# Input projection of a hybrid encoder layer: weights asked for a block ahead, square-sum rows asked for later, pooling products a block later

## The chip, the cores and the metric

The kernel runs on one core of a Trainium2 chip. The metric is the device time of one execution in microseconds (us). The engines are named as in the profile: PE (TensorE, matrix products), PEld (its weight loads), DVE (VectorE), ACT (ScalarE), POOL (GpSimd), SP (SyncE, which here only issues DMAs).

## The reference

One encoder layer over 2048 positions of width 1024: a mixer, a cross-attention into 256 memory rows, and a gated feed-forward part. The change lies in the first part of the mixer, its input projection:

```
z  = rmsnorm(x) @ w_in + b_in          # 2048 x 1024 times 1024 x 2176
za = z[:, :768]      -> gelu, split u and v, rmsnorm of v per head,
                        128-position gating with w_s       (gMLP heads)
zb = z[:, 768:1024]  -> centred average pooling, 4 windows, minus zb,
                        then @ w_pool, + b_pool, * pool_scale
zc = z[:, 1024:]     -> q, k, v of the dilated window attention
```

Everything is float32. A float32 product is made of three products: each operand is split into a rounded high part and a low part (the rest), and high x high, high x low and low x high are added up.

## The kernel before, in words

`mix_in` is the input projection. The positions are cut into 4 chunks `c` of 512. For each chunk the scaled input, transposed, lies in `hth` and `htl` (high and low part, `load_x`). The columns of `w_in` are worked off in this order, where 0 to 7 are blocks of 128 columns (`t_block`) and `None` stands for the 384 columns of the attention's v (`v_rows`):

```
ORDER = ((0, 1, 4, 7, 3, 6, 2, 5, None), (0, 1, 4, 7, None, 3, 6, 2, 5))
```

The first tuple is chunk 0's, the second that of chunks 1 to 3; `b` is the place in it. Blocks 0 and 1 are the pooling heads, 2 to 7 q and k. The gMLP products (`za`) stand in front of place 0 in chunks 1 to 3 and in front of place 7 (`ZB`) in chunk 0. One block is 24 products on PE (8 steps over the 1024, three products each, L115, L116 and L117 in `mm3`: `wth` x `hth`, `wth` x `htl`, `wtl` x `hth`).

A block's weights come in three steps: SP issues a DMA of 512 KB into `st` (two buffers), POOL makes the high part `wth` (L95), DVE the low part `wtl` (L99). `wth` and `wtl` have two buffers each (`a_wt`), so the weights of one block take the place of those of the block two loads earlier, and POOL's L95 waits until PE has done the last product with them. The eight gMLP weight tiles `wa10` to `wa13` and `wa00` to `wa03` come the same way, through the same `st`, but stay (`load_gmlp`).

A block's result `pz` (five PSUM buffers) is multiplied by the spread norms `rb` on DVE and gets its bias on ACT (`t_out`). `rb` comes from the sums of squares of the rows of x (`row_squares`: four DMAs of 512 KB into `xr`, which has two buffers, squared on ACT) by way of `stats`: a reciprocal root on DVE, four products `pt<-diag,ones` on PE (L87), a copy on ACT.

Pooling of a quarter of a chunk pair (`pooling`: DMA of `z`, sums on POOL, split into `pzsh` and `pzsl`) is written one place ahead of its six products `pp` (`pooled`).

Each engine works its own instructions in a fixed order. That order is not the order of the code: a scheduler lays the program out from its own estimates and from the buffers, and `tc.issue_after(x)` marks work that it may not put ahead of instruction x. So the tables below show the order that came out.

Of the kernel before, what the change touches and what calls it, by code (L numbers as in the profile page):

```python
# [12 lines left out]
AF = mybir.ActivationFunctionType  # L13
# [106 lines left out]
class Ffn:  # L120
# [160 lines left out]
    ORDER = [f + v for f in range(0, NF, 2) for v in (0, NF)]  # L281
# [278 lines left out]
ZB = 7  # L560
ORDER = ((0, 1, 4, 7, 3, 6, 2, 5, None), (0, 1, 4, 7, None, 3, 6, 2, 5))
# [3 lines left out]
def mix_in(cx, x_r, x_t, gn, w_t, b_t, w_v, b_v, w_a, b_a, v_g, w_s, b_s, rel, onehot, mrow, tt, pw, pb, psc, edge, invw, zt, vt, yt):  # L565
# [4 lines left out]
    tc, nc = cx.tc, cx.nc  # L570
    AH = 6
    AW = 384
    with ExitStack() as es:
# [6 lines left out]
        wtp = pool("a_wt", 2)  # L580
# [12 lines left out]
        def load_w(pl, tag, src, n=D, **k):  # L593
            st = stp.tile([P, D], F32, name="st", tag="st")
            nc.sync.dma_start(st[:, :n], src)
            return cx.split_w(pl, st[:, :n], tag, tag, n, **k)

        def load_x(c):

            cs = slice(c * 512, (c + 1) * 512)  # L600

            xs = hp.tile([P, KD, 512], F32, name="xs", tag="hth") if c == 0 else None
            hi = hp.tile([P, KD, 512], F32R, name="hth", tag="hth")
            lo = hp.tile([P, KD, 512], F32R, name="htl", tag="htl")
            for k in range(KD):
                xt = xp.tile([P, 512], F32, name="xt", tag="xt") if c else xs[:, k]
                nc.sync.dma_start(xt, x_t[k * P:(k + 1) * P, cs])
                last = nc.scalar.activation(hi[:, k], xt, AF.Copy, scale=gk[:, k:k + 1])
                nc.vector.scalar_tensor_tensor(lo[:, k], xt, gk[:, k:k + 1], hi[:, k].bitcast(F32),
                                               op0=ALU.mult, op1=ALU.subtract)  # L610
            with tc.issue_after(last.ins):
                ss = row_squares(c)
            return (hi, lo), ss

        def row_squares(c):

            ss = sm.tile([P, 4], F32, name="ss", tag="ss4")
            for j in range(4):
                s0 = c * 512 + j * P
                xr = sqp.tile([P, D], F32, name="xr", tag="xr")  # L620
                nc.sync.dma_start(xr, x_r[s0:s0 + P])
                nc.scalar.activation(xr, xr, AF.Square, accum_out=ss[:, j:j + 1])
            return ss

        def stats(ss):

            r = cx.rsqrt(sm, ss, 4, D, "x")
            pt = pst.tile([P, 512], F32, name="pt", tag="pt")
            cx.spread(sm, pt, r)
            rb = hp.tile([P, 512], F32, name="rb", tag="rb")  # L630
            nc.scalar.activation(rb, pt, AF.Copy)
            return r, rb

        def t_block(b, ht, w=None):
            wh, wl = w or load_w(wtp, "wt", w_t[b])
            pz = ps.tile([P, 512], F32, name="pz", tag="pz")
            for k in range(KD):
                sl = slice(k * P, (k + 1) * P)
                cx.mm3(pz, (wh[:, sl], wl[:, sl]), (ht[0][:, k], ht[1][:, k]), k == 0, k == KD - 1)
            return pz  # L640

        def t_out(c, b, pz, rb):

            d = DIL[(b - 2) % 3] if b >= 2 else 1
            n = 512 // d
            zr = evp.tile([P, 512], F32, name="zr", tag="zr")
            nc.vector.tensor_tensor(zr, pz, rb, op=ALU.mult)
            z = evp.tile([P, d, n], F32, name="zt", tag="zt")
            nc.scalar.activation(z, zr.rearrange("p (l r) -> p r l", r=d), AF.Identity, bias=bt[:, b:b + 1])
            nc.scalar.dma_start(zt[b].rearrange("p (r l) -> p r l", r=d)[:, :, c * n:(c + 1) * n], z)  # L650

        def v_rows(c, ht, r):

            bv = evp.tile([P, 512], F32, name="bv", tag="zt")
            nc.sync.dma_start(bv[:, :AW], b_v.to_broadcast([P, AW]))
            pz = [ps.tile([P, 512], F32, name="pz", tag="pz") for _ in range(4)]
            for q in range(4):
                w = [t.rearrange("p (k c) -> p k c", k=2) for t in load_w(wtp, "wt", w_v[:, q * 768:(q + 1) * 768], 768)]
                for j in range(4):
                    sl = slice(j * P, (j + 1) * P)  # L660
                    for k in (2 * q, 2 * q + 1):
                        cx.mm3(pz[j][:, :AW], (ht[0][:, k, sl], ht[1][:, k, sl]), tuple(t[:, k % 2] for t in w),
                               k == 0, k == KD - 1)
            for j in range(4):
                z = evp.tile([P, 512], F32, name="zv", tag="zr")
                nc.vector.scalar_tensor_tensor(z[:, :AW], pz[j][:, :AW], r[:, j:j + 1], bv[:, :AW], op0=ALU.mult, op1=ALU.add)
                nc.scalar.dma_start(vt[c * 512 + j * P:c * 512 + (j + 1) * P, :], z[:, :AW])
# [133 lines left out]
        def load_gmlp():  # L801
            ba = one.tile([P, 2 * AW], F32, name="ba")
            nc.sync.dma_start(ba, b_a.to_broadcast([P, 2 * AW]))
            for i in (1, 0):
                for q in range(4):
                    load_wa(i, q)
            vg = one.tile([P, AW], F32, name="vg")
            nc.sync.dma_start(vg, v_g.to_broadcast([P, AW]))
            bs = one.tile([P, AH], F32, name="bs")
            nc.sync.dma_start(bs, b_s)  # L810
            return ba, vg, bs, load_w(one, "ws", w_s, AH * P)

        todo, ready, held, turns = [], [], [], []
        w0 = load_w(wtp, "wt", w_t[0])
        ht, ss = load_x(0)
        bt = pp.tile([P, 8], F32, name="bt")
        nc.sync.dma_start(bt, b_t)
        st = None
        for c in range(4):
            g = nxt = None  # L820
            for b, blk in enumerate(ORDER[c > 0]):
                if b == (ZB if c == 0 else 0):
                    if c == 0:
                        ba, vg, bs, ws = load_gmlp()
                    g = za(c, ht, st[0])
                if blk is None:
                    v_rows(c, ht, st[0])
                else:
                    held.append((c, blk, t_block(blk, ht, w0 if c == b == 0 else None)))
                if c == 0 and b == SB:  # L830
                    with tc.issue_after(cx.mm.ins):
                        st = stats(ss)
                if st:
                    for a in held:
                        t_out(*a, st[1])
                    held = []
                if b == 4 and c < 3:
                    nxt = load_x(c + 1)
                if b == (ZB + 1 if c == 0 else 2):
                    f = gate(c, *g)  # L840
                    turns = [(f, i) for i in range(4)]
                for _ in range(4 if c == 0 else b >= TB):
                    if turns:
                        f, i = turns.pop(0)
                        with tc.issue_after(cx.split.ins):
                            f(i)
                if b == 6 and c == 1:
                    bias_rows()
                if c == 0 and b == 6:
                    pparams = [pool_params(i) for i in range(2)]  # L850

                if 3 <= b <= 6:
                    done = [q for q in range(S // PN) if 2 * c - 1 <= q < (2 * c + 1 if c < 3 else 2 * c + 2)]
                    for q in done[b - 3:b - 2]:
                        if q >= 0:
                            todo.append(q)
                for a in ready:
                    pooled(*a)
                ready = []
                if b >= (6 if c == 0 else 4) and todo:  # L860
                    q = todo.pop(0)
                    ready = [(q, [pooling(i, q) for i in range(2)])]
            if nxt:
                ht, ss = nxt
                st = stats(ss)

# [379 lines left out]
class OutProj:  # L1248
# [17 lines left out]
    def load_w(self, pl, tag, src, st=None):  # L1266
        t = (st or self.st).tile([P, D], F32, name="st", tag="st")
        self.cx.nc.sync.dma_start(t, src)
        return self.cx.split_w(pl, t, tag, tag, D)
# [213 lines left out]
def body(tc, x_r, x_t, gmix, w_t, b_t, w_v, b_v, w_a, b_a, v_g, w_s, b_s, rel, oh, mrow, pw, pb, psc, edge, invw, mem, mem_t, gm, w_kv, w_qt,  # L1483
         w_o, gmem, w_out, b_out, b_o, w_up, b_up, conv, w_down, b_down, gffn, gfin, out):
    with tc.tile_pool(name="const", bufs=1) as const, tc.tile_pool(name="scratch", bufs=1, space=DRAM) as dr:
# [9 lines left out]
        x2_d = dr.tile([D, S], F32, name="x2_d")  # L1495
        act_d = dr.tile([NF, P, S], F32, name="act_d")
        mix_in(cx, x_r, x_t, gmix, w_t, b_t, w_v, b_v, w_a, b_a, v_g, w_s, b_s, rel, oh, mrow, tt, pw, pb, psc, edge, invw, zt, vt, yt)
        late, es, eo = ExitStack(), ExitStack(), ExitStack()
        proj = []
# [66 lines left out]
```

## Time and profile before

| | before |
|---|---|
| three runs, us | 2547.81, 2548.83, 2554.39 (median 2548.83) |
| the profiled execution, own time | 2544.94 us |
| its span, first to last instruction | 2542.2 us |
| PE busy | 2468.8 us, 97% of the span |
| DVE, ACT, POOL busy | 1802.3, 1000.7, 956.3 us |
| mean granted TensorE clock | 0.985 of 2.4 GHz |

The times are of whole executions; the trace is of one of them, and 2.7 us of it lie outside the span. The input projection takes the first 420 us of the span, with the keys and values of the memory rows and the attention behind it. A granted clock of 1.00 is 2.4 GHz, one of 0.50 is 1.2 GHz, and a value in between is a mean over a stretch that has both.

### The profile page before, as it was taken

Reading aid. Unit: us, or ns where it says so; the run is one execution under the profiler, and the core shown is the slowest. Engines: PE = TensorE matmul, PEld = TensorE weight load, DVE = VectorE, ACT = ScalarE, POOL = GpSimd, SP = SyncE. Lnnn points to the kernel's source line nnn. Section 1 sums busy time; section 2 is a strip of 40 time slices with the busy share of each in tenths; the row PEclk is TensorE's granted clock in tenths of the full one; section 3 lists DMA queues with packets and bytes.
Section 4 is the critical chain, followed back from the end, with each engine's and each line's share of the span. In section 5 each row is a group of like instructions: output and inputs, shape, how many; then the busy total and the mean of one; then the engine's idle time right before and its main releaser. Section 6 shows DMA issues by size and latency. Waiting matters only on the chain. (4 is left out here: it accounts for less than half of the span.)

```text
span 2542.2 us, 33993 instructions
## 1 busy us (share of the span) xinstructions
PE 2468.8 (97%) x12454; PEld 2110.3 (83%) x12454; DVE 1802.3 (71%) x2658; ACT 1000.7 (39%) x1524; POOL 956.3 (38%) x805
## 2 busy tenths in 40 slices
PE   8999998899999999998999999999999999999998
PEld 6998897898887899987888888877888887888886
DVE  5575747868647867676888887877888887645453
ACT  4122112666212233234444444544444444444442
POOL 3211315673204223266555554025555553210000
PEclk9999998999999999999999999999999999999998
DMA  9444527775662222232222222762222223767673
GB/s 301 131 133 152 156 66 241 227 236 190 203 206 89 71 71 69 65 108 94 85 81 76 90 79 95 233 230 91 83 90 76 79 88 122 259 219 233 215 235 117
DMA packets 220095, 361.57 MB, mean 142 GB/s; under 512 B 38828, under 2 KB 104472, under 8 KB 219928
## 3 DMA queue, kind: packets, MB, share of 16 engines
q1 hardware_dynamic: 155980, 286.83, 35.8%
q10 hardware_dynamic: 63948, 72.58, 8.2%
q8 instruction: 97, 1.59, 0.3%
q14 instruction: 70, 0.57, 0.1%
HBM read 280.61 MB, written 79.90 MB: 142 GB/s over the span
## 5 line engine op out<-in xcount | busy, mean ns | idle before, releaser
L403 DVE TENSOR_TENSOR w<-dr,w 128x1024 fp32r<-128x1024 f32 x176 | 220.4, 1261 | 169.8 <-ACT w L402 164.6
L116 PE MATMUL pd<-w 128*128 128x512 f32 x704 | 275.5, 391 | 1.6 <-DVE w L403 1.6
L117 PE MATMUL pd<-w 128*128 128x512 f32 x704 | 275.1, 391 | 0.0
L402 ACT ACTIVATE w<-dr 128x1024 fp32r<-128x1024 f32 x176 | 185.0, 1058 | 218.2 <-PE pd L117 202.0
L115 PE MATMUL pd<-w 128*128 128x512 f32 x704 | 260.2, 392 | 0.7 <-ACT rb L538 0.7
L116 PE MATMUL py<-htl,w 128*128 128x512 f32 x528 | 208.7, 395 | 0.0
L115 PE MATMUL py<-hth,w 128*128 128x512 f32 x528 | 207.2, 394 | 0.8 <-DVE u L371 0.8
L117 PE MATMUL py<-hth,w 128*128 128x512 f32 x528 | 206.2, 394 | 0.0
L315 DVE SCALAR_TENSOR_TENSOR t<-u,vec,t 128x1022 f32<-128x1022 f32 (+1 forms) x88 | 134.3, 1526 | 70.3 <-ACT t L314 48.1
L314 ACT ACTIVATE t<-u,vec 128x1022 f32<-128x1022 f32 (+1 forms) x88 | 109.5, 1245 | 160.0 <-DVE u L364 141.2
L116 PEld LDWEIGHTS pd<-w 128*128 128x128 f32 x704 | 132.7, 188 | 30.3 <-DVE w L403 3.2
L115 PEld LDWEIGHTS pd<-w 128*128 128x128 f32 x704 | 132.4, 188 | 28.0 <-ACT rb L538 0.9
L117 PEld LDWEIGHTS pd<-w 128*128 128x128 f32 x704 | 132.6, 188 | 27.4
L115 PE MATMUL px<-hth,w 128*128 128x512 f32 x352 | 140.0, 398 | 6.3 <-ACT w L265 4.7
L95 POOL TENSOR_SCALAR wth<-st 128x1024 fp32r<-128x1024 f32 (+1 forms) x48 | 49.5, 1031 | 251.7 <-PE pz L116 173.3
L462 POOL TENSOR_TENSOR q<-q 128x512 f32<-128x512 f32 x24 | 39.2, 1634 | 276.8 <-ACT q L458 275.6
L117 PE MATMUL px<-hth,w 128*128 128x512 f32 x352 | 139.6, 397 | 3.1 <-DVE w L266 3.1
L116 PE MATMUL px<-htl,w 128*128 128x512 f32 x352 | 140.0, 398 | 0.0
L116 PE MATMUL pz<-htl,w 128*128 128x512 f32 x352 | 139.1, 395 | 0.0
L117 PE MATMUL pz<-hth,w 128*128 128x512 f32 x352 | 139.0, 395 | 0.1
L115 PE MATMUL pz<-hth,w 128*128 128x512 f32 x352 | 138.6, 394 | 0.0
L316 DVE SCALAR_TENSOR_TENSOR t<-u,vec,t 128x1022 f32<-128x1022 f32 (+1 forms) x88 | 136.2, 1547 | 0.1
(716 smaller groups left out, 7130.9 us busy)
## 6 DMA issues: line engine op xcount, KB each, us to landing
dr<-act_d SPq DMA_DIRECT2D x176, 256.0 KB, 3.9
dr<-in_w_down_dram SPq DMA_DIRECT2D x176, 256.0 KB, 4.2
wa<-in_w_up_dram SPq DMA_DIRECT2D x44, 512.0 KB, 3.2
wb<-in_w_up_dram SPq DMA_DIRECT2D x44, 512.0 KB, 3.3
st<-in_w_t_dram SPq DMA_DIRECT2D x32, 512.0 KB, 4.1
xt<-in_x_t_dram SPq DMA_DIRECT2D x56, 256.0 KB, 3.9
act_d<-t ACTq DMA_DIRECT2D x22, 513.0 KB, 3.1
act_d<-t ACTq DMA_DIRECT2D x22, 511.0 KB, 3.1
```

Of the source, the lines that this page charges most:

```text
L95: nc.gpsimd.tensor_scalar(hi, src, 1.0, 1.0, op0=ALU.mult, op1=ALU.mult)
L115: mm(out, a[0], b[0], start=start, stop=False, skip_group_check=again)
L116: mm(out, a[0], b[1], start=False, stop=False, skip_group_check=again)
L117: self.mm = mm(out, a[1], b[0], start=False, stop=stop, skip_group_check=again)
L314: nc.scalar.activation(t, u[:, 1:n + 1], AF.Identity, bias=vec[:, 4, f:f + 1], scale=vec[:, 2, f:f + 1])
L315: nc.vector.scalar_tensor_tensor(t, u[:, 0:n], vec[:, 1, f:f + 1], t, op0=ALU.mult, op1=ALU.add)
L316: nc.vector.scalar_tensor_tensor(t, u[:, 2:n + 2], vec[:, 3, f:f + 1], t, op0=ALU.mult, op1=ALU.add)
L402: nc.scalar.activation(hl[:, 0], t, AF.Copy)
L403: nc.vector.tensor_tensor(hl[:, 1], t, hl[:, 0].bitcast(F32), op=ALU.subtract)
L462: nc.gpsimd.tensor_tensor(sq[0], sq[0], q, op=ALU.add)
```

## The change

Three edits in `mix_in`. (1) In chunk 0 the second block's weights are asked for right behind the first chunk's input, and inside a chunk each block loads the weights of the block behind it before its own products are written; `row_squares` is taken out of `load_x`. (2) The rows for `row_squares` of chunk c+1 are written at place 7 of chunk 0 (behind `load_gmlp`) or place 5 of chunks 1 and 2, and not with the input at place 4; only the squaring on ACT is kept behind the input's last activation, no longer the DMA. (3) The products `pooled` stand one more place behind their `pooling`.

```diff
-            with tc.issue_after(last.ins):
-                ss = row_squares(c)
-            return (hi, lo), ss
-
-        def row_squares(c):
+            return (hi, lo), last
+
+        def row_squares(c, last):
...
                 nc.sync.dma_start(xr, x_r[s0:s0 + P])
-                nc.scalar.activation(xr, xr, AF.Square, accum_out=ss[:, j:j + 1])
+                with tc.issue_after(last.ins):
+                    nc.scalar.activation(xr, xr, AF.Square, accum_out=ss[:, j:j + 1])
...
-        todo, ready, held, turns = [], [], [], []
+        todo, ready, parts, held, turns = [], [], [], [], []
         w0 = load_w(wtp, "wt", w_t[0])
-        ht, ss = load_x(0)
+        ht, last = load_x(0)
+        wt = [load_w(wtp, "wt", w_t[ORDER[0][1]])]
+        ss = row_squares(0, last)
...
-                    held.append((c, blk, t_block(blk, ht, w0 if c == b == 0 else None)))
+                    w, w0 = w0, None
+
+                    after = (ORDER[c > 0] + ORDER[1])[b + 1] if c < 3 or b < len(ORDER[1]) - 1 else None
+                    if wt:
+                        w0 = wt.pop()
+                    elif after is not None and not (b == 0 and c) and b + 1 != (ZB if c == 0 else len(ORDER[1])):
+                        w0 = load_w(wtp, "wt", w_t[after])
+                    held.append((c, blk, t_block(blk, ht, w)))
...
+                if b == (ZB if c == 0 else 5) and nxt:
+                    ss = row_squares(c + 1, nxt[1])
...
-                for a in ready:
+
+                for a in parts:
                     pooled(*a)
-                ready = []
+                parts, ready = ready, []
...
+        for a in parts + ready:
+            pooled(*a)
```

No instruction of an engine is added or taken away; from the 3881st product on, PE's order is that of before. Three places show what moves.

SP, at the start of the program, before (`st` is a block's weights, `xs` and `xt` the input, `xr` the rows for the squares):

```order
L591 DMA gk<-in_gmix_dram 128x8
L595 DMA st<-in_w_t_dram 128x1024
L607 DMA xs<-in_x_t_dram 128x512 x8
L621 DMA xr<-in_x_r_dram 128x1024 x2
L817 DMA bt<-in_b_t_dram 128x8
L595 DMA st<-in_w_t_dram 128x1024 x2
L607 DMA xt<-in_x_t_dram 128x512 x5
```

SP, the same place, now:

```order
L591 DMA gk<-in_gmix_dram 128x8
L595 DMA st<-in_w_t_dram 128x1024
L607 DMA xs<-in_x_t_dram 128x512 x8
L595 DMA st<-in_w_t_dram 128x1024
L619 DMA xr<-in_x_r_dram 128x1024 x2
L818 DMA bt<-in_b_t_dram 128x8
L595 DMA st<-in_w_t_dram 128x1024
```

The second block's weights have moved ahead of the two row tiles; nothing else in this stretch has.

PE, in chunk 0 from the last products of block 7 on, the difference cut to its first rows (`pt<-diag,ones` are the four products that spread the norms; `x4` is their count):

```order
 L115 MATMUL pz<-hth,wth 128x512
 L116 MATMUL pz<-htl,wth 128x512
+L117 MATMUL pz<-hth,wtl 128x512
+L115 MATMUL pz<-hth,wth 128x512
+L116 MATMUL pz<-htl,wth 128x512
```

and its last rows, 21 products later:

```order
+L115 MATMUL pz<-hth,wth 128x512
+L116 MATMUL pz<-htl,wth 128x512
 L87 MATMUL pt<-diag,ones 128x128 x4
-L117 MATMUL pz<-hth,wtl 128x512
-L115 MATMUL pz<-hth,wth 128x512
```

The spread stood at the start of the fifth block (block 3, 26 products ahead of block 6, the sixth), and now stands at its end, one product ahead of block 6.

PE, chunk 1, from the end of block 0 (`pz_1384`, weights `wth_1380`) to the products behind it, before; `pz_1420` is block 1:

```order
L115 MATMUL pz_1384<-hth_392,wth_1380 128x512
L116 MATMUL pz_1384<-htl_393,wth_1380 128x512
L117 MATMUL pz_1384<-hth_392,wtl_1381 128x512
L115 MATMUL pz_1420<-hth_392,wth_1416 128x512
L116 MATMUL pz_1420<-htl_393,wth_1416 128x512
L117 MATMUL pz_1420<-hth_392,wtl_1417 128x512
L115 MATMUL pz_1420<-hth_392,wth_1416 128x512
```

PE, the same place, now; `pz_1426` is block 1 and `pz_1462` block 4, whose weights `wth_1416` were loaded first:

```order
L115 MATMUL pz_1384<-hth_398,wth_1380 128x512
L116 MATMUL pz_1384<-htl_399,wth_1380 128x512
L117 MATMUL pz_1384<-hth_398,wtl_1381 128x512
L115 MATMUL pz_1426<-hth_398,wth_1422 128x512
L116 MATMUL pz_1426<-htl_399,wth_1422 128x512
L115 MATMUL pz_1462<-hth_398,wth_1416 128x512
L116 MATMUL pz_1462<-htl_399,wth_1416 128x512
```

POOL, the three splits that belong to this place, before (`waits` are the semaphores that the instruction waits for):

```order
L95 TENSOR_SCALAR wth_1380<-st_1378 128x1024 [waits DMAHW3_49,DVE_49,PE_49]
L95 TENSOR_SCALAR wth_1416<-st_1414 128x1024 [waits DMAHW4_49,DVE_49,PE_49]
L95 TENSOR_SCALAR wth_1452<-st_1450 128x1024 [waits DMAHW5_49,DVE_49,PE_49]
L95 TENSOR_SCALAR wth_1519<-st_1517 128x1024 [waits DMAHW1_49,DVE_49,PE_49]
L750 TENSOR_TENSOR s0_1748<-z_1746 128x271 [waits DMAHW7_49,DMAHW3_49]
```

and now:

```order
L95 TENSOR_SCALAR wth_1380<-st_1378 128x1024 [waits DMAHW1_49,DVE_49,PE_49]
L95 TENSOR_SCALAR wth_1416<-st_1414 128x1024 [waits DMAHW4_49,DVE_49,PE_49]
L95 TENSOR_SCALAR wth_1422<-st_1420 128x1024 [waits DMAHW5_49,DVE_49,PE_49]
L749 TENSOR_TENSOR s0_1735<-z_1733 128x271 [waits DMAHW3_49,DMAHW2_49]
L749 TENSOR_TENSOR s1_1737<-s0_1735 64x269 [waits Pool_49]
```

Before, the split behind block 0's (`wth_1416`) was block 1's own, and the third one (`wth_1452`, into the buffer that block 0's weights leave) was for the block behind. Now the second is for block 4, the block behind, and the third, into the buffer that block 0's weights leave, is block 1's own.

PE, at the end of chunk 3, before: the last of the four blocks behind `v_rows` (`pz_3732`, which ends them) and the keys and values of the memory rows (`pt_3921`, from the memory rows `mh`, `ml` and the weights `kwh`, `kwl`):

```order
L115 MATMUL pz_3732<-hth_2602,wth_3728 128x512
L116 MATMUL pz_3732<-htl_2603,wth_3728 128x512
L117 MATMUL pz_3732<-hth_2602,wtl_3729 128x512
L115 MATMUL pt_3921<-mh_3867,kwh_3917 128x256
L116 MATMUL pt_3921<-ml_3868,kwh_3917 128x256
```

PE, the same place, now, at the end of the first 22 products of `pt_3921`; `pz_3676` and `pz_3719` are the last two of the four blocks:

```order
L115 MATMUL pt_3921<-mh_3867,kwh_3917 128x256
L115 MATMUL pz_3676<-hth_2602,wth_3582 128x512
L116 MATMUL pz_3676<-htl_2603,wth_3582 128x512
L116 MATMUL pt_3921<-ml_3868,kwh_3917 128x256
L117 MATMUL pt_3921<-mh_3867,kwl_3918 128x256
L115 MATMUL pt_3954<-mh_3867,kwh_3950 128x256
```

The first two of the four blocks still stand in front of `pt_3921`; the other two, 48 products, now lie among and behind its products and those of `pt_3954`.

## Rows read from the trace of the kernel before

**Rows 1.** The page, its head and its first part

```profile
span 2542.2 us, 33993 instructions
...
PE 2468.8 (97%) x12454; PEld 2110.3 (83%) x12454; DVE 1802.3 (71%) x2658; ACT 1000.7 (39%) x1524; POOL 956.3 (38%) x805
```

**Rows 2.** Windows of the span, busy time by engine, granted clock, DMA share

```profile
core 0: us, PE busy (x) PEld busy (x) DVE busy (x) ACT busy (x) POOL busy (x), PEclk, DMA share, GB/s
...
15.00:25.00 10.00, 8.28 (x24) 6.11 (x25) 6.61 (x12) 6.03 (x11) 3.88 (x4) 0.66 0.95 314
...
55.00:65.00 10.00, 6.24 (x26) 4.90 (x25) 6.42 (x11) 4.40 (x4) 6.44 (x9) 0.83 0.84 233
...
160.00:395.00 235.00, 235.00 (x1236) 214.08 (x1235) 149.47 (x241) 47.19 (x62) 63.39 (x72) 1.00 0.47 138
395.00:420.00 25.00, 20.97 (x92) 16.42 (x90) 16.72 (x24) 3.14 (x4) 13.28 (x14) 1.00 0.71 175
420.00:440.00 20.00, 13.55 (x71) 11.73 (x71) 19.81 (x24) 9.31 (x19) 13.62 (x13) 0.74 0.86 275
```

**Rows 3.** PE's waits from 0 to 64 us: us in total, times, longest us

```profile
PE pz L115 <- POOL wth L95: 2.8, 1, 2.8
...
PE pz L116 <- DVE wa12l L99: 0.8, 1, 0.8
PE pp L115 <- POOL z L740: 0.8, 1, 0.8
PE pp L116 <- DVE pzsl L99: 0.7, 1, 0.7
```

**Rows 4.** SP's DMA issues, by timeline: start us, us, engine, line [idle before]

```profile
6.31 1.05 SPq L621 DMA_DIRECT2D xr<-in_x_r_dram  x2
...
8.65 1.06 SPq L595 DMA_DIRECT2D st<-in_w_t_dram  x2
```

**Rows 5.** POOL's timeline: high parts and one low part (L99)

```profile
15.59 1.04 POOL L95 TENSOR_SCALAR wth<-st 128x1024 fp32r<-128x1024 f32 x1 [9.57 <-DMA st<-in_w_t_dram]
...
157.84 1.05 POOL L95 TENSOR_SCALAR wth<-st 128x1024 fp32r<-128x1024 f32 x1 [38.62 <-PE pz L116]
...
194.01 1.05 POOL L95 TENSOR_SCALAR wth<-st 128x1024 fp32r<-128x1024 f32 x1 [0.72 <-POOL s L750]
...
393.73 2.39 POOL L99 TENSOR_TENSOR kwl<-st,kwh 128x1024 fp32r<-128x1024 f32 x1
```

**Rows 6.** PE's timeline: single products at six places

```profile
16.69 0.80 PE L115 MATMUL pz<-hth,wth 128*128 128x512 f32 x1 [2.79 <-POOL wth L95]
...
36.55 0.83 PE L87 MATMUL pt<-diag,ones 128*128 128x128 f32 x6
...
157.59 0.39 PE L117 MATMUL pz<-hth,wtl 128*128 128x512 f32 x1
157.81 0.39 PE L115 MATMUL pz<-hth,wth 128*128 128x512 f32 x1
...
193.69 0.39 PE L115 MATMUL pz<-hth,wth 128*128 128x512 f32 x1
...
400.65 0.50 PE L117 MATMUL pz<-hth,wtl 128*128 128x512 f32 x1 [1.70 <-DVE wtl L99]
```

**Rows 7.** ACT's and DVE's timelines: the spread norms and their first use

```profile
37.64 0.60 ACT L631 ACTIVATE rb<-pt 128x512 f32<-128x512 f32 x1 [1.91 <-PE pt L87]
...
38.27 1.29 DVE L647 TENSOR_TENSOR zr<-pz,rb 128x512 f32<-128x512 f32 x2 [2.81 <-ACT rb L631]
```

**Rows 8.** PE's waits from 64 to 398 us

```profile
PE pz L115 <- POOL wa00h L95: 1.5, 1, 1.5
```

**Rows 9.** PE's waits from 398 to 480 us

```profile
PE pz L117 <- DVE wtl L99: 3.3, 2, 1.7
PE pt L116 <- DVE ml L1175: 2.9, 2, 1.5
...
PE pp L115 <- POOL z L742: 1.9, 1, 1.9
```

More of the change, by code (lines that the diff above doesn't have):

```diff
@@ L863, in mix_in @@
             if nxt:
-                ht, ss = nxt
+                ht, _ = nxt
                 st = stats(ss)
+        for a in parts + ready:
+            pooled(*a)
 MJ = 2
```

## The prediction

> **What bounds the kernel now.** The page's first part [rows 1] gives PE 97% of the span, so a change is worth what it does to PE's idle time and to PE's clock, and nothing else. The next view to read is therefore PE's waits, stretch by stretch, and beside it the windows with the granted clock. They show three regimes in the 420 us of the input projection.
>
> At the start PE waits for what arrives: 2.8 us for the second block's `wth`, then four waits between 55 and 65 us [rows 3, 8]. The windows have the DMA engines at 0.95 and 0.84 there, and the granted clock at 0.66 from 15 to 25 us: PE idles before 16.69, and then part of the stretch runs at 1.2 GHz, the lower level [rows 2, 6]. From 64 to 398 us there is one wait, of 1.5 us, right at the beginning [rows 8]; the window 160 to 395 is 235.00 of 235.00 busy at clock 1.00 [rows 2]. In this middle there is nothing to win by an earlier weight, and anything made late shows in full. From 395 to 440 PE is idle for 25 - 20.97 + 20 - 13.55 = 10.5 us, and the clock of 0.74 in its second half costs 20 x 0.26 = 5.2 us more [rows 2]. The waits there that touch the change are of three kinds: for a low part `wtl`, for a pooling tile, and for the memory rows `ml` [rows 9].
>
> **Start of the program.** SP issued the second block's weights at 8.65, behind two row tiles issued at 6.31 [rows 4]. Moved ahead of them, the issue comes 2.3 us earlier. If the landing moves with it, POOL's split, which began at 15.59 on the landing, begins at 13.2 and ends at 14.3 [rows 5]. PE's wait of 2.8 then shrinks to about 0.4; I take 1.0, because DVE's low part comes behind POOL's high part and PE needs it two products later: -1.8. The stretch at 1.2 GHz behind that wait costs 10 x 0.34 = 3.4 us [rows 2]; with the wait nearly gone I take it as gone: -3.4.
>
> Against that stands the spread of the norms, which the scheduler has moved from 26 products ahead of block 6 to one ahead. Block 6 is the sixth, and there are five `pz` buffers: it needs one that `t_out` has emptied. In the trace the spread's products start at 36.55, ACT's copy runs from 37.64 to 38.24, and the first of two products with it on DVE ends near 38.27 + 0.65 = 38.9 [rows 6, 7]: 2.35 us from the spread to a free buffer. Behind the spread's start PE has 0.83 us of its own and one product of 0.23. About 1.3 us are left: +1.2 to +1.3. These sum to -4.0.
>
> The gain must survive the DMA-bound stretch up to 65 us. The order of issues puts two row tiles of chunk 1 (1 MB) behind the first gMLP weights instead of ahead of them; at the 314 GB/s of the window 15 to 25 [rows 2] this is 3.3 us. Here the change does only part of what it says: SP still issues row tiles among the gMLP weights, wherever `xr` has a free buffer. The pooling products, now one tile later, leave the places of the waits for `pzsl` and `z` but stand next to `wa12l`, which PE waits for too [rows 3]; I take that as nothing. So **start: -4.0**, from -1 (all of it eaten by the full DMA engines) to -7 (no wait before block 6, no clock loss, and the pooling waits gone).
>
> **Six blocks whose own weights now come second.** In chunks 1 to 3 nothing is loaded ahead at place 0 or over `v_rows`. So at places 1 and 5 the code loads the next block's weights first and the block's own behind them. There are two buffers: the next block gets the free one, and the block's own weights get the one that the products directly in front still read. The order of PE and POOL shows exactly that: before, 24 products or more lay between the release of a buffer and the first use of what is put into it, and now one or two.
>
> The price stands in the trace of before, for the same buffer released by the same product: POOL's split of 157.84 began on PE's release and took 1.05 us, to 158.89 [rows 5]. PE takes 0.06 us to start behind a split (15.59 + 1.04 = 16.63, start 16.69 [rows 5, 6]). The first product of the block behind started at 157.81 [rows 6]. With the block's own weights in that split, PE stands from 157.81 to 158.95: **1.14 us**. The low part doesn't add to it, for the 22 to 24 products of the next block stand right behind the first two. At place 5 the release is by the last product of `v_rows`: POOL's split there ran from 194.01 to 195.06, and PE's next block started at 193.69: **1.43 us** [rows 5, 6]. Three times each: 3 x 1.14 + 3 x 1.43 = **+7.7**. Below, +6, if POOL starts a little sooner behind a shorter wait; above, +10, where sums of the pooling stand ahead of such a split on POOL (in chunk 3 four of them do). At the other places where a block's weights come earlier now, the gain is nothing: the cover was 24 products x 0.227 = 5.4 us (a product starts 0.22 to 0.23 us behind the last [rows 6]) against the 1.05 us of POOL's part and about as much for DVE's, and no wait is listed [rows 8].
>
> **End of chunk 3.** The last two blocks move into and behind the products of the memory rows. The two waits for `wtl`, 3.3 us [rows 9], came because POOL had a low part `kwl` of 2.39 us [rows 5] ahead of a split. The first two blocks have their weights before that; the last two now have `kwl` ahead of them: I leave the 3.3 where it is. The wait of 1.9 for `z` [rows 9] goes, since the products stand a place later: -1.9. PE reaches the memory rows' products 48 products, 10.9 us, sooner, and has those 48 to fill the waits behind. The chain that makes `ml` is one of DMA and DVE, which the blocks don't drive; I take that the fill gives back a third of the 5.2 us of half clock: -1.7. **End: -3.6**, from -12 (of 15.7 us idle and at half clock only the 3.3 stay) to +9 (PE stands for the memory rows for the 10.9 us that the four blocks covered, less 1.9). These ends are far apart, since the trace has no execution in that order; I stay near the rows that I can name.
>
> **Sum.** -4.0 + 7.7 - 3.6 = +0.1. On the profiled execution's 2544.94 that is 2545.0, 2.7 of it outside the span; the median of the runs is 3.9 above that execution: **2549**. What a measurement of this kernel can tell from no change is about 0.3%, 7.6 us.
>
> **Rivals.** *The start and the end win (faster).* The start keeps 7 of its gain, the last two blocks fill most of the holes behind 420 us for 10, the six waits cost 6: -11, 2538. For it: the products moved behind the memory rows are just what PE lacks from 420 to 440, with 13.55 of 20 us busy. Against it: both splits for them queue behind `kwl`. Chance 0.31.
>
> *The six waits take the clock with them (slower).* Each wait drops PE to 1.2 GHz. The window 15 to 25 loses 3.4 us to that, behind a wait of 2.8. Six times 3.4 on top of 7.7 is +28, less 7.6: about +20, 2569. It decides as soon as any of the six is followed by a stretch below 1.00. The trace speaks against it: two waits for `wtl`, together 3.3 us, the first of them 1.70 us up to 400.65, lie in the window 395 to 420, and that has a clock of 1.00 [rows 2, 6, 9]. The Trainium skill speaks for it: "TensorE: Matmul & The Clock Gate", section "HAM oscillation — how this bites in real kernels", tells of a kernel whose weights were waited for ahead of every short batch of products and which fell back to half rate each time. The trace agrees with that rule only where waits crowd, as from 55 to 65 us (clock 0.83); the six lie tens of us apart. Chance 0.06.
>
> *PE arrives too early at the memory rows (slower).* The products of `pt_3921` stand in front of the last two blocks, and PE does its work in order: if `mh` is not there PE stands, with 48 products ready behind it. At 9 us for it the sum is +12.7, about 2561; it decides from about 7.5 us on. For it: `ml` was already waited for in the old order, 10.9 us later [rows 9]. Against it: what is in front of that chain on DVE and SP moves ahead as well. Chance 0.17.
>
> *The start does nothing (same).* The DMA engines were full, so what PE saves at 16 us it waits at 60 us; with -0.5 for the start the sum is +3.6, 2552. Chance 0.12.
>
> **Numbers.** My own sum 0.34, the last rival 0.12: same 0.46. Faster 0.31. Slower 0.06 + 0.17 = 0.23. The likeliest case by itself runs from 2542 to 2556; the range takes in the faster rival and nearly all of the one at 2561: **2536 to 2561**.
>
> **What would show it.** Right: the second block starts near 14 us and the clock stays 1.00 from 15 to 25; a wait of about 1.3 us stands ahead of block 6, for `zr`; PE lists six waits for `wth` between 150 and 400 us, 1.1 to 1.5 each, and the window 160 to 395 is no longer full, yet at clock 1.00. Wrong: a clock below 1.00 there, a wait above 3 us for `mh` near 410, or no waits for `wth` at all. The least certain step is the end of chunk 3, whose sign I can't fix.

## The result and the profile after

The changed kernel takes 2581.48 us (median of four runs, 2579.54 to 2582.59) against 2549.49 for the kernel before: ratio 1.0124, 95% interval 1.0104 to 1.0143. It is slower by 32 us, and lies outside the predicted range.

The head and the first part of its page, to set beside [rows 1]:

```profile
span 2579.6 us, 34005 instructions
...
PE 2480.9 (96%) x12454; PEld 2115.9 (82%) x12454; DVE 1816.5 (70%) x2658; ACT 999.3 (39%) x1524; POOL 958.0 (37%) x805
```

The span is 37.4 us longer than the traced one of before, with the same work; the 12 instructions more are semaphore instructions. Windows of the changed kernel, with the columns of [rows 2]:

```profile
15.00:25.00 10.00, 9.47 (x42) 7.49 (x42) 6.30 (x9) 5.47 (x9) 3.26 (x4) 1.00 0.95 329
55.00:65.00 10.00, 6.58 (x22) 5.65 (x21) 7.20 (x14) 4.96 (x5) 5.76 (x9) 0.66 0.87 234
160.00:395.00 235.00, 225.41 (x1157) 202.35 (x1156) 137.81 (x214) 44.47 (x58) 58.17 (x66) 0.99 0.40 118
198.00:202.00 4.00, 3.88 (x10) 3.12 (x11) 3.91 (x7) 0.00 (x0) 0.47 (x2) 0.57 0.67 245
307.00:311.00 4.00, 3.19 (x8) 2.57 (x9) 3.91 (x7) 0.00 (x0) 0.76 (x1) 0.57 0.81 268
413.00:417.00 4.00, 4.00 (x12) 3.16 (x11) 3.88 (x8) 0.00 (x0) 3.30 (x3) 0.57 1.71 234
395.00:420.00 25.00, 21.46 (x105) 19.33 (x104) 22.40 (x41) 2.30 (x4) 14.67 (x16) 0.93 0.93 222
420.00:440.00 20.00, 11.22 (x49) 9.41 (x48) 13.84 (x18) 3.99 (x9) 7.54 (x6) 0.75 0.36 113
```

The reader is to see two things. The start is better: clock 1.00 from 15 to 25 us where it was 0.66. And the middle, 235.00 of 235.00 busy before, has lost 9.6 us, with three short stretches in it or right behind it at a mean clock of 0.57.

To see where the time went, three marks on PE's timeline divide the span: the first product of the block at place 7 of chunk 0 (93.51 us in before's trace), the first of the block behind chunk 3's `v_rows` (392.85), and the first product `pl<-am0h` of the cross-attention (769.21). This gives a start, the middle of the projection, the stretch with the memory rows, the attention and the output product, and a rest. Each entry is the distance of two marks in one trace, in us; the kernels of the lower rows are those of the next section.

| trace | start | middle | behind chunk 3's `v_rows` | rest |
|---|---|---|---|---|
| before | 93.5 | 299.3 | 376.4 | 1773.0 |
| before, a second trace | 98.2 | 299.3 | 382.7 | 1770.2 |
| changed | 93.4 | 318.3 | 397.4 | 1770.6 |
| second weights early alone (two traces) | 95.1, 95.7 | 299.3, 299.3 | 378.0, 376.5 | 1770.9, 1773.7 |
| pooling products later alone | 99.5 | 299.9 | 385.0 | 1770.5 |
| no loading ahead in chunks 1 to 3 | 95.7 | 300.1 | 384.8 | 1770.1 |
| own weights first | 93.7 | 299.8 | 390.2 | 1772.6 |
| own first, chunks 0 to 2 | 94.3 | 299.7 | 382.1 | 1771.1 |
| loading ahead alone | 93.7 | 311.1 | 387.2 | 1768.4 |
| exchange, chunks 1 to 3 | 98.1 | 310.9 | 392.7 | 1770.7 |
| exchange, chunk 1 | 95.0 | 303.4 | 382.0 | 1771.2 |
| exchange, chunk 3 | 96.2 | 302.9 | 395.4 | 1770.7 |
| exchange and pooling later | 95.2 | 317.6 | 388.8 | 1770.6 |

The changed kernel loses 19.0 us in the middle and 15 to 21 behind it, depending on which trace of before stands beside it. The start and the rest give nothing in this trace.

**The middle.** PE's waits in it, in the changed kernel (total, times, longest):

```profile
PE pz L115 <- POOL wth L95: 12.6, 6, 4.8
PE pz L116 <- DVE wtl L99: 1.5, 2, 0.8
```

These are the six blocks whose own weights come second. On PE's timeline they are 0.96 us each at place 1, and 2.09, 4.81 and 2.77 at place 5. The longest one, in chunk 2, on PE:

```profile
302.49 0.33 PE L116 MATMUL pz<-wtl,hth 128*128 128x384 f32 x1
302.66 0.34 PE L117 MATMUL pz<-wth,htl 128*128 128x384 f32 x1
307.81 0.80 PE L115 MATMUL pz<-hth,wth 128*128 128x512 f32 x1 [4.81 <-POOL wth L95]
```

and on POOL in the same time:

```profile
300.14 0.64 POOL L749 TENSOR_TENSOR s<-z 128x271 f32<-128x271 f32 x1 [2.81 <-DMA z<-zt]
300.86 1.35 POOL L749 TENSOR_TENSOR s<-s 128x269 f32<-128x269 f32 x2
302.17 1.05 POOL L95 TENSOR_SCALAR wth<-st 128x1024 fp32r<-128x1024 f32 x1
303.30 2.43 POOL L749 TENSOR_TENSOR s<-s 64x257 f32<-64x257 f32 x1
306.34 0.41 POOL L95 TENSOR_SCALAR pzsh<-s 128x256 fp32r<-128x256 f32 x1 [0.61 <-DVE s L758]
306.71 1.05 POOL L95 TENSOR_SCALAR wth<-st 128x1024 fp32r<-128x1024 f32 x1
```

PE is done with `v_rows` at 302.66 + 0.34 = 303.0. POOL has just split the next block's weights (302.17). Then its order has a sum of the pooling, 2.43 us, and a split `pzsh` that waits for DVE; only at 306.71 does it come to the block's own weights. PE starts at 307.81, and its first product takes 0.80 us instead of 0.39: the half clock of the window 307 to 311. The windows behind the other two waits of place 5 show the same. Each of the three loses at most 4 x 0.43 = 1.7 us, since PE was still waiting in part of the second window (3.19 us busy of 4.00); the third lies behind the mark that ends the middle.

In chunk 3 POOL's part is different. Three sums stand ahead of the split, then it waits for its DMA, and the split itself takes 1.71 us instead of 1.05:

```profile
407.40 2.16 POOL L749 TENSOR_TENSOR s<-s 128x269 f32<-128x269 f32 x3
409.91 1.71 POOL L95 TENSOR_SCALAR wth<-st 128x1024 fp32r<-128x1024 f32 x1 [0.35 <-DMA st<-in_w_t_dram]
```

The list of waits is not the whole price. A listed wait counts from the end of the product before, 0.3 to 0.4 us behind its start, but without a wait the next product would have started 0.17 to 0.23 us behind that start: 302.66 and 307.81 lie 5.15 us apart, 302.49 and 302.66 lie 0.17 apart, so PE starts 4.98 us late behind a wait listed as 4.81. In starts, the six places cost 3 x 1.12 + 2.25 + 4.98 + 2.94 = 13.5 us, the two waits for `wtl` 1.8, and the two stretches at half clock inside the middle about 3.1 (1.7 and 1.4). That is 18.4 of the 19.0 us.

**Behind chunk 3's `v_rows`.** PE's longest waits of the changed kernel from 411.7 to 809 us:

```profile
PE pt L115 <- DVE kvl L1203: 5.0, 2, 2.8
PE pt L115 <- ACT mh L1187: 4.6, 1, 4.6
PE pt L116 <- DVE ml L1188: 4.2, 3, 1.5
PE pl L115 <- ACT q L979: 3.8, 1, 3.8
PE pt L115 <- ACT ev L1230: 3.0, 2, 2.1
PE pt L115 <- DVE xt L1303: 2.9, 3, 2.1
```

Beside [rows 9] the waits for `wtl` and `z` are gone, and that for `mh`, before

```profile
PE pt L115 <- ACT mh L1174: 0.7, 1, 0.7
```

has grown to 4.6. No wait is large beside 15 to 21 us: the loss is spread. It does not begin at once. The first 42 us behind the mark, before and now, the one of 4.6 for `mh` included:

```profile
392.85:435.00 42.15, 32.95 (x142) 26.34 (x142) 33.63 (x48) 11.50 (x20) 24.05 (x25) 0.88 0.78 217
...
411.67:454.00 42.33, 33.55 (x149) 28.11 (x150) 30.71 (x42) 6.79 (x12) 25.69 (x22) 0.84 0.67 175
```

PE gets through 149 products now and 142 before, so up to there nothing is lost on balance; all of the loss comes in the 355 us behind.

### The profile page after: what moved, and what is told of

Read it like the earlier page. It is cut to its first block, busy times and chain, and to the rows that moved or that the text cites. A ratio compares the mean times of both kernels' runs of the same rounds, so it can differ in the third digit from the quotient of the medians.

```text
span 2579.6 us, 34005 instructions
## 1 busy us (share of the span) xinstructions
PE 2480.9 (96%) x12454; PEld 2115.9 (82%) x12454; DVE 1816.5 (70%) x2658; ACT 999.3 (39%) x1524; POOL 958.0 (37%) x805
```

## The experiments

Ten kernels besides before itself, one of them timed twice, all compared with before on the same chip. The differences are given to before, except where another kernel is named. The expectations speak of five theories: A, the order of the two loads at the six blocks makes the loss in the middle; B, the DMA queue or POOL's pooling sums make it; C, the order that the scheduler chose behind chunk 3 makes the second loss; D, the later pooling products make it; E, whatever is late in the middle comes back several times behind it.

**Own weights first.** The changed kernel, but a block without weights loads its own before the next block's:

```diff
-                    w, w0 = w0, None
+                    w, w0 = w0 or load_w(wtp, "wt", w_t[blk]), None
```

> The changed kernel, but at every place a block without weights loads its own before it loads the next block's. Theory A (the six blocks whose own weights come second cost about 18 us, waits of 12.7 us and three stretches at 1.2 GHz): no wait for wth between 150 and 410 us, clock 1.00 there, and the block behind v_rows of chunk 3 about 18 us sooner than in the changed kernel; 2563 us if the products of the memory rows and the attention (420 to 760 us) lose as much as in the changed kernel, 2548 if they don't. Rival B (the middle's waits come from the DMA queue or from POOL's pooling sums, not from the order of the two loads): waits for wth of over 5 us in all remain and the time stays above 2572.

Measured: 2559.84 us, ratio 1.0035 (1.0022 to 1.0047). The six waits are gone, the middle is 299.8, and of the 1.24% that the changed kernel is slower, 0.35% are left. With own weights first none of the middle's loss is left, so theory A holds and B falls as a cause by itself. But the stretch behind still takes 390.2: there is a second loss.

**No loading ahead in chunks 1 to 3.** The changed kernel with

```diff
-                    elif after is not None and not (b == 0 and c) and b + 1 != (ZB if c == 0 else len(ORDER[1])):
+                    elif after is not None and c == 0 and b + 1 != (ZB if c == 0 else len(ORDER[1])):
```

> The changed kernel without loading ahead in chunks 1 to 3; chunk 0's start, the rows and the pooling products stay as changed. Theory A: the six waits are gone as with own weights first, 2548 to 2563, and equal to it within 5 us up to 410 us. Rival B: waits for wth remain. Beside it, a theory C (the loss behind 420 us comes from the order into which the scheduler puts the memory rows' products, whichever edit shifts it): the loss there differs from both kernels, without any edit to that part.

Measured: 2551.53, ratio 1.0004 (0.9987 to 1.0021). Middle 300.1, the stretch behind 384.8: no loss beyond about 0.2% is left, so it hangs on the loading ahead in chunks 1 to 3, though it isn't all in the middle.

**Pooling products later alone.** The kernel before with the third edit:

```diff
-                for a in ready:
+                for a in parts:
                     pooled(*a)
-                ready = []
+                parts, ready = ready, []
...
+        for a in parts + ready:
+            pooled(*a)
```

> The kernel before with the third edit alone, pooling products one place later. If the later pooling products cost nothing in the projection and only the order behind 420 us makes the second half of the loss: no new wait up to 410 us. Theory C: the loss behind 420 us is anywhere from 0 to 18 us, 2549 to 2567. Rival D (the later pooling products themselves make the loss behind 420 us, since two groups of them now stand at the end of chunk 3): plus 15 to 18 us, 2564 to 2567, with waits of PE for z there.

Measured: 2551.11, ratio 1.0000 (0.9983 to 1.0018). Rival D falls: alone, the third edit costs and brings nothing beyond 0.2%.

**Loading ahead alone.** The kernel before with the first edit, but not with its gain at the start: `row_squares` is still inside `load_x`, so the second block's weights are asked for behind the row tiles, and PE waits 2.71 us for them, nearly as before.

```diff
         ht, ss = load_x(0)
+        wt = [load_w(wtp, "wt", w_t[ORDER[0][1]])]
...
-                    held.append((c, blk, t_block(blk, ht, w0 if c == b == 0 else None)))
+                    w, w0 = w0, None
+                    after = (ORDER[c > 0] + ORDER[1])[b + 1] if c < 3 or b < len(ORDER[1]) - 1 else None
+                    if wt:
+                        w0 = wt.pop()
+                    elif after is not None and not (b == 0 and c) and b + 1 != (ZB if c == 0 else len(ORDER[1])):
+                        w0 = load_w(wtp, "wt", w_t[after])
+                    held.append((c, blk, t_block(blk, ht, w)))
```

> The kernel before with the loading ahead alone (first edit without moving the rows and without the later pooling products). Theory A: the six waits and the three stretches at 1.2 GHz are all there, plus 15 to 20 us by 410 us. With theory C the loss behind 420 us is open, 2564 to 2582; with rival D it is absent, 2564 to 2568.

Measured: 2567.57, ratio 1.0068 (1.0043 to 1.0093). The six waits are there, but with 0.96, 1.25, 0.96, 1.25, 0.96 and 2.12 us they make 7.5 us, and no stretch at half clock follows them up to the end of chunk 3. The middle takes 311.1, 11.8 us more than before, where theory A had said 15 to 20: the longer waits at place 5 and the half clock are missing. They came with another edit.

**The exchange, chunks 1 to 3.** The kernel before, with nothing but the two loads exchanged at the six places:

```diff
-                    held.append((c, blk, t_block(blk, ht, w0 if c == b == 0 else None)))
+                    w, w0 = w0, None
+                    if c and b in (1, 5):
+                        w0 = load_w(wtp, "wt", w_t[ORDER[1][b + 1]])
+                    held.append((c, blk, t_block(blk, ht, w)))
```

> The kernel before, with one thing: at places 1 and 5 of chunks 1 to 3 the next block's weights are loaded ahead of the block's own. Theory A at the size that the prediction gave: six waits for wth, 0.96 each at place 1 and 1.2 to 2.1 at place 5, 7 to 8 us together, clock 1.00 behind them, and the end of chunk 3's v_rows blocks 7 to 10 us later. The pooling products stand as before, so no sums of the pooling wait in front of the split: the long waits of 2.1, 4.8 and 2.8 us of the changed kernel are absent. In all 2557 to 2562 if the order behind 420 us costs little.

Measured: 2573.72, ratio 1.0104 (1.0078 to 1.0130). This alone makes most of the slowdown. Its waits in the middle (110 to 413 us, with two of 0.3 that belong to other places), and a window behind the place 5 of chunk 1 and of chunk 2:

```profile
PE pz L115 <- POOL wth L95: 7.9, 8, 1.9
...
201.00:205.00 4.00, 3.29 (x14) 2.74 (x15) 3.90 (x6) 0.00 (x0) 2.46 (x3) 1.00 0.78 231
307.00:311.00 4.00, 4.00 (x18) 3.33 (x19) 3.90 (x7) 0.00 (x0) 1.04 (x2) 1.00 0.80 193
```

The clock is 1.00 here; behind the third place 5, a wait of 1.94, it was 0.51 for three microseconds, which was not expected:

```profile
410.00:413.00 3.00, 3.00 (x9) 2.30 (x8) 2.90 (x6) 0.00 (x0) 3.00 (x3) 0.51 1.27 336
```

The middle is 11.6 us longer than before, more than the 7 to 10 expected and more than the six waits, which make 7.3. PE's first wait at place 1:

```profile
162.17 0.39 PE L117 MATMUL pz<-hth,wtl 128*128 128x512 f32 x1
163.52 0.50 PE L115 MATMUL pz<-hth,wth 128*128 128x512 f32 x1 [0.96 <-POOL wth L95]
```

The two products start 1.35 us apart instead of 0.23, so PE is 1.12 late. At place 5 it is 1.42, 1.42 and 2.11 late: 8.3 for the six places. The rest, 3.3, is two waits for `wtl` in `v_rows` (1.0 listed), the two waits of 0.3, which before does not have, and slower starts behind all of these. The time was above the 2557 to 2562 expected, and most of the excess lies behind: 392.7.

**The exchange with the later pooling products.** Both edits together on the kernel before.

> The kernel before with the exchange in chunks 1 to 3 and with the later pooling products. With both, POOL has sums of the pooling, in chunk 2 a split of them too, in front of the block's own split at place 5. If that makes the long waits of the changed kernel: at place 5 waits of 2 to 5 us (8 to 10 in all) and a granted clock of 0.50 behind at least two of them, where the kernel with the exchange alone had 1.25, 1.25 and 1.94 us and a clock of 1.00 behind the first two; by the last blocks of chunk 3 4 to 9 us later than that kernel. If the long waits come from the rows or the DMA queue: 1.2 to 2 us each, as without the later pooling products.

Measured: 2574.07, ratio 1.0087 (1.0073 to 1.0101). Waits in the middle, and the windows behind the place 5 of chunks 1 and 2:

```profile
PE pz L115 <- POOL wth L95: 12.1, 6, 4.2
...
201.00:205.00 4.00, 3.96 (x11) 3.10 (x12) 3.91 (x7) 0.00 (x0) 0.40 (x1) 0.58 0.66 242
310.00:314.00 4.00, 3.85 (x11) 3.02 (x12) 3.90 (x7) 0.00 (x0) 0.10 (x1) 0.61 0.54 196
```

At place 5 it waits 3.24, 4.22 and 1.78 us, 9.2 in all, as expected if the sums make the long waits. So the third edit, harmless alone, puts POOL's sums in front of the split that the first edit has made urgent: the middle goes from 310.9 to 317.6, nearly the changed kernel's 318.3. The long waits in chunks 1 and 2 don't come from the rows, which are asked for here as before. The third is shorter than the 2.77 of the changed kernel, whose split in chunk 3 also waited for its DMA.

**The exchange in chunk 1, and in chunk 3.** As above with `c == 1` or `c == 3` for `c`. What they share is two waits; what parts them is that the scheduler, behind chunk 3, keeps before's order in the first and not in the second.

> The kernel before with the two loads exchanged at places 1 and 5 of chunk 1 alone. The order of PE behind the end of chunk 3 is that of before, row by row. Theory A: two waits of 0.96 and about 1.25 us, 2.2 us in all, nothing behind; the same as before within 0.2%. If a wait in the projection grew on its way (theory E: whatever is late there comes back several times behind 420 us), 5 us and more.

> The kernel before with the same exchange in chunk 3 alone: two waits again, 0.96 and 1.9 to 2.1 us, but here the order of PE behind the end of chunk 3 differs from before almost everywhere (37 of 450 rows stand where they stood). Theory C (the order costs): 3 us of waits up to 410 us and 8 to 18 more between 410 and 750 us, 2558 to 2570, 0.4 to 0.8% slower. Theory E, or nothing in the order: within 3 us of the kernel with the exchange in chunk 1.

Measured: chunk 1, 2554.43, ratio 1.0014 (1.0005 to 1.0023); chunk 3, 2570.18, ratio 1.0075 (1.0061 to 1.0089). The waits for `wth` are 0.96 and 1.25 against 0.96 and 1.43, the middle is 303.4 against 302.9, 4.1 and 3.6 us longer than before's. The windows from chunk 3's last blocks to the cross-attention, first that of chunk 1's kernel, then that of chunk 3's:

```profile
398.48:780.48 382.00, 353.77 (x2149) 315.10 (x2149) 261.91 (x616) 163.92 (x435) 167.17 (x116) 0.96 0.68 209
...
399.15:794.54 395.39, 357.49 (x2148) 318.30 (x2149) 271.33 (x611) 163.29 (x435) 169.66 (x115) 0.94 0.65 201
```

The same products on PE, nearly the same share of the DMA engines, 0.68 and 0.65, and 13.4 us more: PE's idle time is 382.00 - 353.77 = 28.2 against 395.39 - 357.49 = 37.9, and it is busy 3.7 us longer for the same products, at a mean clock of 0.94 against 0.96. Theory C holds: the order costs. The table bears it out: the six kernels that load ahead or exchange in chunk 3 take 387.2 to 397.4 us behind `v_rows`, the eight other traces 376.4 to 385.0. Whether PE's own order costs, or that of the DMAs and of POOL that moved with it, isn't parted. Theory E falls, since the waits of chunk 1 come back once and no more.

**Own weights first, no loading ahead in chunk 3.** The other test of theory C, now without any of the six waits:

```diff
-                    after = (ORDER[c > 0] + ORDER[1])[b + 1] if c < 3 or b < len(ORDER[1]) - 1 else None
+                    after = (ORDER[c > 0] + ORDER[1])[b + 1] if c < 3 else None
```

> The changed kernel with own weights first, and loading ahead in chunks 0 to 2 only. Chunks 0 to 2 are then as in the kernel with own weights first; from the end of chunk 3 on PE's order is that of the kernel without loading ahead. Theory C (the order behind 420 us carries the rest of the loss): about 2551, as without loading ahead, 8 us less than with own weights first. If the loss lay in chunks 1 to 3: about 2559, as with own weights first.

Measured: 2549.72, ratio 1.0008 (0.9997 to 1.0020), against 1.0035 with own weights first in all chunks. The middle is 299.7 against 299.8; behind it 382.1 against 390.2. No block waits for its weights in either middle, and the order behind still makes 0.27%, 7 us.

**The second weights early, alone.** The kernel before, with the second block's weights asked for behind chunk 0's input and ahead of the row tiles:

```diff
+            if c == 0:
+                wt.append(load_w(wtp, "wt", w_t[ORDER[0][1]]))
             with tc.issue_after(last.ins):
                 ss = row_squares(c)
...
-                    held.append((c, blk, t_block(blk, ht, w0 if c == b == 0 else None)))
+                    held.append((c, blk, t_block(blk, ht, (w0, wt[0])[b] if c == 0 and b < 2 else None)))
```

> The kernel before with one part of the first edit alone: in chunk 0 the second block's weights are asked for ahead of the row tiles. From the first block of chunk 1 on PE's order is that of before. If the full DMA engines take back what the start gains: the third block about 4 us sooner than before, the eighth group of gMLP products (70 to 80 us) and everything behind it within 2 us of before; 2549 to 2553, the same as before. If the gain lasts: 4 to 5 us less.

Measured: 2544.93, ratio 0.9988 (0.9971 to 1.0005): faster on the whole, but not beyond its interval. So it was timed once more:

> The early second weights alone once more, timed against before in five rounds: 0 to 4 us faster (0.9988 had an interval from 0.9971 to 1.0005). If the full DMA engines take the gain back: within 2 us of before; if a part of it lasts: 3 to 4 us less.

Measured: 2547.50, ratio 0.9985 (0.9976 to 0.9994), 3.8 us less than before's 2551.30 on that chip. This is the one part of the change that is worth keeping: 0.15% faster than before, with an interval from 0.06 to 0.24%.

The second edit, the rows asked for later, was not run alone. Without loading ahead in chunks 1 to 3 it stands beside the early weights and the third edit, and the three together come to 1.0004.

**The kernel before once more.**

> The kernel before once more, for a second trace: by how much two executions of the same program differ, and where. Expected: up to 7 us, in the first 80 us and behind 400 us, where DMAs are waited for, and nothing in the middle of the projection.

Measured: 2552.43. The middle is 299.3 to the tenth, as before; the start differs by 4.7 us, the stretch behind chunk 3 by 6.3.

## Why the prediction was wrong

Two steps failed: the price of the six blocks, and the end of chunk 3, where the stretch behind 440 us was taken as unchanged.

**The start: right in its steps, its size open.** The second block starts at 14.72 (said: near 14), the clock of 15 to 25 us is 1.00, the third block comes 4.1 us sooner, and the price foreseen for the spread is there too, as a wait ahead of block 6 for `zr`. In the changed kernel:

```profile
14.72 0.50 PE L115 MATMUL pz<-hth,wth 128*128 128x512 f32 x1 [0.17 <-POOL wth L95]
...
21.10 0.39 PE L115 MATMUL pz<-hth,wth 128*128 128x512 f32 x1
...
40.11 0.47 PE L115 MATMUL pz<-hth,wth 128*128 128x512 f32 x1 [1.27 <-DVE zr L646]
```

and the third block before:

```profile
25.21 0.39 PE L115 MATMUL pz<-hth,wth 128*128 128x512 f32 x1
```

By the terms it should have come 1.8 + 3.4 = 5.2 us sooner. The 3.4 charged the whole stretch at half clock, though PE was still waiting in 0.9 us of it (15.7 to 16.6). The sum -4.0 was not in the changed kernel's trace, where 0.2 us was left at the first mark. The window 55 to 65, at a clock of 0.66 against 0.83 before, took up to 1.7 us of it; where the rest went isn't shown. The start differs by 4.7 us between two traces of one program, so one trace can't settle it. The six traces with early second weights reach the first mark at 93.4 to 95.7, the eight without at 93.5 to 99.5: 1.5 us sooner on the mean. In the timed runs the early weights alone came out at -3.8 us, with an interval from 1.5 to 6.1. So -4.0 lies within what was measured, and that the DMA-bound stretch takes a good part of the gain is not ruled out.

**The six blocks: right mechanism, wrong size.** The term was 3 x 1.14 + 3 x 1.43 = +7.7; the middle lost 19.0. As lateness of PE's starts, which is how the term was worked out, the exchange alone showed 3 x 1.12 and 1.42, 1.42, 2.11: 8.3, near the term. But the middle lost 11.6 there, since smaller waits for `wtl` and `wth`, which the term did not have, came with them. The step that failed is the one that priced the six waits from the order of before, edit by edit. I named the case where sums of the pooling stand ahead of such a split and kept it for the upper end, +10; the third edit makes it the rule at place 5. In the changed kernel the six waits are 12.6 us as listed, 13.5 in starts.

**The clock: a rival at 0.06 that came half true.** I held two waits of 1.7 and 1.6 us at clock 1.00 against it. Three of the six waits, those at place 5, were longer, and behind each of them PE ran at 1.2 GHz for a while: about 4.8 us together, 3.1 of it in the middle, where the rival had said 3.4 for each of the six. My own row of 15 to 25 us, at 0.66 behind a wait of 2.8, was the nearer one for such waits, and I passed over it in saying that the trace agrees only where waits crowd. The Trainium skill's page "TensorE: Matmul & The Clock Gate", section "HAM oscillation — how this bites in real kernels", tells of half rate behind each wait; there it is the next slice of the right-hand matrix that is waited for, not a block's weights as here. The trace agrees for waits of 2.09, 2.77 and 4.81 us, not for the three of 0.96.

**The end of chunk 3: near enough up to 440 us, and the stretch behind left out.** The term was -3.6, from -12 to +9, and I worked it out for 395 to 440 us. The step that failed is that I took the stretch behind 440 us as unchanged. Up to there the term was not far off: in the first 42 us behind chunk 3's `v_rows` PE does 149 products now and 142 before. But the scheduler had laid out the next 350 us anew, and this order is slower by 15 to 21 us. The exchange in chunk 3, and own weights first with and without chunk 3, show that it is the order and not what waits in front. The wait of over 3 us for `mh`, which I had named as a sign against my forecast, is there with 4.6 us, but it lies in the 42 us that lose nothing on balance, and it is 3.3 us in the kernel that loads own weights first without chunk 3, whose 382.1 us behind are no more than before's:

```profile
PE pt L115 <- ACT mh L1187: 3.3, 1, 3.3
```

The loss is spread over later waits, for `kvl`, `q`, `ev` and `xt` among others, and a mean clock of 0.94 against 0.96. Which of the moved groups would have to go back to regain it wasn't tried. The rival on `mh` was also summed in two ways: 9 us for it took the place of the -3.6 (+12.7), but the 7.5 us from which it decides leaves the -3.6 in; without it the rival decides from 3.9 us on.

**The sum.** -0.2 at the start, +19.0 in the middle, +21.0 behind, -2.4 in the rest: +37.4 between the two traces; with the second trace of before -4.9, +19.0, +14.7 and +0.4: +29.1. The 32 us of the medians lie between.

## What to carry to other kernels

With two buffers, a load for the next tile that is written ahead of the tile's own load takes the free buffer and leaves the own load the one still being read; count the products between the release and the first use at each place, not only at the typical one. Read how late PE starts, not only the waits listed: here 7.3 us of waits at six places went with 11.6 us in the middle. Price edits together where they meet on one engine's queue: here two that cost 11.6 and 0.6 us in the middle cost 18.3 together. And where a scheduler lays out the program, read its order as far as it differs, not as far as the edit reaches; about half of this loss lay where no line was changed.

## What the runs showed of the hardware

Two executions of one program agreed to 0.1 us over 299.3 us in which PE waited for nothing, and differed by 4.7 us in the first 94 us and by 6.3 us behind, where PE has waits. A difference of that size in a single trace is no evidence.

Behind single waits of PE in a stretch that was otherwise full, the granted clock stayed at 1.00 after 0.96, 1.25 and 1.43 us, and went to 0.50 for a while after 2.09, 2.77, 3.24, 4.22 and 4.81 us. Around 2 us it went either way: down after 1.94 in the exchange of chunks 1 to 3 and after 1.78 in the exchange with the later pooling products, but 1.00 from 405 to 412 us in the kernel with loading ahead alone, behind its wait of 2.12:

```profile
405.00:412.00 7.00, 7.00 (x32) 5.78 (x32) 5.03 (x6) 0.00 (x0) 5.42 (x4) 1.00 1.02 126
```
